# A decoder layer's weight preparation in one copy and one subtraction per 2048-column unit

## The chip, the core and the metric

The kernel runs on one core of a Trainium2 chip. The metric is the device time of one execution in microseconds. Times come from separate executions; the profile comes from one further execution, whose own time is given beside them.

## The reference

One decoder layer over 256 tokens with 2048 channels, in float32. Cut to what matters:

```python
proj = x @ w_in                       # 2048 -> GLA q,k,v,gate,rank | FoX q,k,v,forget | two merge gates
y_gla = gated_linear_attention(...) @ w_branch_gla        # 4 heads, chunked, RMSNorm, silu gate
y_fox = forgetting_attention(...) @ w_branch_fox          # 8 heads, softmax with log-forget bias
merged = sigmoid(ma) * y_gla + sigmoid(mb) * y_fox
x = layer_norm(ALPHA * x + merged @ w_out, ln1_g, ln1_b)
h = gelu(causal_dwconv(x @ w_gate, conv_w, conv_b)) * (x @ w_up)     # 2048 -> 5632
x = layer_norm(ALPHA * x + h @ w_down, ln2_g, ln2_b)                 # 5632 -> 2048
x = x + sigmoid(x @ w_ple_gate) * (p @ w_ple_proj)
```

All the large weights are read from HBM once, and all the large products have 256 rows.

## The kernel before, in words

**Arithmetic.** A float32 weight is not multiplied as it is. ScalarE (ACT) copies it into the fp32r type, which keeps fewer bits; this is `hi`. VectorE (DVE) subtracts `hi` from the raw weight; this is `lo`. TensorE (PE) then forms hi x activation-hi, hi x activation-lo and lo x activation-hi. Activations are split in the same way.

**Units.** The large weights are laid out as 284 units of 128 x 2048 float32 (1 MB), in the order in which PE uses them. `prep()` (L92) prepares the next unit: for each of its two halves of 1024 columns it takes a `raw` tile, issues the load on SyncE's queue (SP, L98), and has the half copied by ACT (L100, which the profile shows as L76, the line of the helper `copy`) and subtracted by DVE (L102). `unit()` (L110) hands the next unit to the matmuls after it has called `prep()` until the two units behind it are prepared too, so three units are in hand.

**The ring.** The pool `ring` holds `raw`, `hi` and `lo`. Before, each slot is half a unit: four slots of `raw`, six each of `hi` and `lo`. Two other kinds of tile use the raw slots: `maskf0` and `maskf1` at the start (L157; GpSimd, POOL, casts them into an 8-bit mask) and the four `praw` tiles of the embedding projection (`ple_prep`, L716). The first stage, the FoX value projection (`fv`, L285), has eight wider units of its own (`fv_prep`, L263: halves of 1048 columns), in the same three kinds of slots.

**Order.** SP's instructions, the loads, run in program order (L78). For the other engines a planner orders the instructions, by data dependence, slot release and priorities, when the kernel is built. The order on each engine can change with any edit. The engines then run their own streams in order and wait for one another by semaphores.

**Stages, in order of PE's work, with the tile that each writes:** `fv` (3 banks for each of two token blocks); `psfq`/`psfk`, `psq`/`psk` (units 0 to 31, one output block of 128 channels per unit or half unit), with the gate blocks `psg<head>` from `gla_gates` (L370) between; `gv` and `gr` (units 32 to 63; `x_half`, L213); `psm` (64 to 95); `psa`/`psb` (96 to 119); `wo` (120 to 135); `psg`/`psu` (136 to 223, the MLP's gate and up projections, L779); `dn` (224 to 267); `pg` (268 to 283). The stages `psfq` to `psb`, `psg` and `psu` go through `w_unit` (L163): per 128 columns of weight a 512-column matmul with `hi` (L169) and a 256-column one with `lo` (L171). `gv`, `gr`, `wo`, `dn`, `pg` go through `x_mm` (L186), with the weight as the moving operand. The output of such a stage is made in two halves of 1024 channels. PSUM has six banks for these stages (`pmm`) and two for transposes and small products (`pmx`).

**The seam after wo and dn.** The last two units of each are the tail: both are kept, and the four banks (two token blocks times two 512-column blocks) are finished one after another. As each ends, DVE adds the residual into `z` (L695) and takes statistics (L696). `ln_out` (L654) then combines the statistics (L659 to L662, with a power on POOL), normalises `z` in four parts (L667 on DVE, L670 on ACT), transposes them on PE into `ptl` (L673), applies gain and bias to each 128 x 128 block into `lny` (L680 on ACT and L682 on DVE in turn) and splits them into hi (L76) and lo (L685) of `x1T`, the next stage's activation. While this runs PE has the matmuls of the embedding projection, `pp` (`ple_proj`, L735). `affine` (L700) applies gain and bias (tiles `lnb`) to the untransposed `z` in 16 steps (L704, L706), between the MLP's units in program order.

**The middle of wo and dn.** `mid1` (L746) and `mid2` (L812) issue the loads of two `z` tiles and two `lnb` tiles, 1 MB each, on SP's queue between the loads of units; `ple_prep` issues the `praw` loads near the end of the same stages.

Of the kernel before, what the change touches and what calls it, by code (L numbers as in the profile page):

```python
# [9 lines left out]
F32 = mybir.dt.float32  # L10
F32R = mybir.dt.float32r
# [3 lines left out]
ALU = mybir.AluOpType  # L15
# [4 lines left out]
P = 128  # L20
# [12 lines left out]
NS = 1048  # L33
# [12 lines left out]
def tile_block(ctx: ExitStack, tc: tile.TileContext, wu, wfv, wpp, xT_in, x_in, pT_in, wlr,  # L46
               chan, gnorm, lng, ident_in, mask_in, cmask_in, sel_in, out):
    nc = tc.nc

    cst = ctx.enter_context(tc.tile_pool(name="cst", bufs=1))  # L50
    ring = ctx.enter_context(tc.tile_pool(name="ring", bufs=6))
    big = ctx.enter_context(tc.tile_pool(name="big", bufs=14))
    sm = ctx.enter_context(tc.tile_pool(name="sm", bufs=2))
    early = ctx.enter_context(ExitStack())
# [5 lines left out]
    def s8(shape, dt=F32, name=None):  # L60
        return big.tile(shape, dt, tag="S8", name=name)

    def t1(name):
        return sm.tile([P, 256], F32, tag="t1", bufs=6, name=name)

    def t2(name):
        return sm.tile([P, 512], F32, tag="t2", bufs=6, name=name)
# [7 lines left out]
    def copy(o, i, scale=1.0):  # L75
        nc.scalar.activation(o, i, AF.Copy, bias=0.0, scale=scale)  # L76
# [13 lines left out]
    ready = {}  # L90

    def prep():  # L92
        u = n_prep[0]
        n_prep[0] += 1
        his, los = [], []
        for h in range(2):
            raw = ring.tile([P, 1024], F32, tag="raw", bufs=4, name=f"raw{u}_{h}")
            nc.sync.dma_start(raw, wu[u, :, h * 1024:(h + 1) * 1024])  # L98
            hi = ring.tile([P, 1024], F32R, tag="hi", name=f"hi{u}_{h}")
            copy(hi, raw)  # L100
            lo = ring.tile([P, 1024], F32R, tag="lo", name=f"lo{u}_{h}")
            nc.vector.tensor_tensor(lo, raw, hi.bitcast(F32), ALU.subtract)  # L102
            his.append(hi)
            los.append(lo)
        ready[u] = (his, los)

    n_used = [0]
    NU = wu.shape[0]
# [1 line left out]
    def unit():  # L110
        u = n_used[0]
        n_used[0] += 1
        while n_prep[0] < min(NU, u + 3):
            prep()
        return ready.pop(u)
# [4 lines left out]
    def load_x(g, k0, k1, step=2):  # L120
        for k in range(k0, k1, step):
            e = slice(k, k + step)
            raw = t2("xraw").rearrange("p (k t) -> p k t", t=S)[:, 0:step, :]
            nc.sync.dma_start(raw, xT_in[:, 4 * g + k:4 * g + k + step, :])
            copy(xT[g][:, e, 0:256], raw)
            nc.vector.tensor_tensor(xT[g][:, e, 256:512], raw,
                                    xT[g][:, e, 0:256].bitcast(F32), ALU.subtract)
# [20 lines left out]
    def load_consts():  # L148
        nc.sync.dma_start(ident, ident_in)
        nc.sync.dma_start(chn, chan)  # L150
        nc.sync.dma_start(sel, sel_in)
        nc.sync.dma_start(cmask, cmask_in)

    def load_consts2():
        nc.sync.dma_start(gnb, gnorm.broadcast_to([P, 512]))
        for i in range(2):
            maskf = ring.tile([P, 4, 256], F32, tag="raw", bufs=4, name=f"maskf{i}")  # L157
            nc.sync.dma_start(maskf, mask_in[:, 8 * i:8 * i + 8, :].rearrange(
                "p (l t) n -> p l (t n)", t=2))
            nc.gpsimd.tensor_copy(mask[:, 4 * i:4 * i + 4, :], maskf)  # L160
# [99 lines left out]
    fch = ((0, 352), (352, 352), (704, 344))  # L260
    fbk = [[mmtile(f"fv_{t}{c}") for c in range(3)] for t in range(2)]

    def fv_prep(u, hs=(0, 1), his=None, los=None):  # L263
        his, los = his or [], los or []
        for h in hs:
            raw = ring.tile([P, NS], F32, tag="raw", bufs=4, name=f"fvraw{u}_{h}")
            hi = ring.tile([P, NS], F32R, tag="hi", name=f"fvhi{u}_{h}")
            lo = ring.tile([P, NS], F32R, tag="lo", name=f"fvlo{u}_{h}")
            for o, n in fch if u == 0 else ((0, NS),):
                e = slice(o, o + n)  # L270
                nc.sync.dma_start(raw[:, e], wfv[u, :, h, e])
                copy(hi[:, e], raw[:, e])
                nc.vector.tensor_tensor(lo[:, e], raw[:, e], hi[:, e].bitcast(F32), ALU.subtract)
            his.append(hi)
            los.append(lo)
        return his, los

    load_x(0, 0, 1, 1)
    f0 = fv_prep(0, (0,))
    load_x(0, 1, 2, 1)  # L280
    fvu = [fv_prep(0, (1,), *f0)]
    load_x(0, 2, 4)
    fvu.append(fv_prep(1))
    load_x(1, 0, 4)
    for u in range(8):  # L285
        hi, lo = fvu[u]
        for j in range(2):
            kt = 2 * u + j
            a = xT[kt // 4][:, kt % 4, :]
            for cs in ((0,), (1,), (2,)) if u == 0 else ((0, 1, 2),):  # L290
                for t in range(2):
                    ah, al = a[:, t * P:t * P + P], a[:, 256 + t * P:256 + t * P + P]
                    for i, (w, x) in enumerate(((hi[j], ah), (lo[j], ah), (hi[j], al))):
                        for c in cs:
                            o, n = fch[c]
                            nc.tensor.matmul(fbk[t][c][:, 0:n], lhsT=x, rhs=w[:, o:o + n],  # L296
                                             start=kt == 0 and i == 0,
                                             stop=kt == 15 and i == 2)
        if u + 2 < 8:
            fvu.append(fv_prep(u + 2))  # L300
        if u == 1:
            load_x(2, 0, 4)
        elif u == 2:
            load_x(3, 0, 4)
        elif u == 4:
            load_consts()
# [95 lines left out]
    fq = s8([P, 8, 256], name="fq")  # L402
    fk = s8([P, 8, 256], name="fk")
    load_consts2()
    for nm, dst, sc in (("fq", fq, P ** -0.5), ("fk", fk, 1.0)):
        for n in range(8):
            hi, lo = unit()
# [56 lines left out]
    for nm, dst, sc in (("q", gq, 1.0 / 16.0), ("k", gk, 1.0)):  # L464
        for n in range(8):
            hi, lo = unit()
            ps = mmtile(f"ps{nm}{n}")
            w_unit(ps, hi, lo, xT, range(16), True, True)
            h, c = n // 2, n % 2
# [141 lines left out]
    for n in range(32):  # L611
        hi, lo = unit()
# [14 lines left out]
    for n in range(16):  # L627
        hi, lo = unit()
# [5 lines left out]
        j = n % 2  # L634
# [81 lines left out]
    def ple_prep(half):  # L716

        w = [s8([P, 2048], F32R, name=f"pw{half}{i}") for i in range(2)]
        pt_ = s8([P, 2, 512], F32R, name=f"pTs{half}")
        pTs = [pt_[:, k, :] for k in range(2)]  # L720
        for k in range(2):
            raw = ring.tile([P, 1024], F32, tag="raw", bufs=4, name=f"praw{half}{k}")
            nc.sync.dma_start(raw, wpp[half, :, k * 1024:k * 1024 + 1024])
            o = slice(k * 1024, k * 1024 + 1024)
            copy(w[0][:, o], raw)
            nc.vector.tensor_tensor(w[1][:, o], raw, w[0][:, o].bitcast(F32), ALU.subtract)
        pT = t2("pTr").rearrange("p (k t) -> p k t", t=S)
        nc.sync.dma_start(pT, pT_in)
        for k in range(2):
            copy(pTs[k][:, 0:256], pT[:, k, :])  # L730
            nc.vector.tensor_tensor(pTs[k][:, 256:512], pT[:, k, :],
                                    pTs[k][:, 0:256].bitcast(F32), ALU.subtract)
        return w, pTs
# [20 lines left out]
    def done1(t):  # L754
        if t == 1:
            pb.extend(ple_proj(0, *pq[0]))
        ln_out(z1, st1, t, x1T, c_g1, c_b1, "l1", P_LN1[t])

    residual("wo", mT, 16, z1, st1, (mid1, lambda: pq.append(ple_prep(0))), done1)
    for t in range(2):  # L760
        for c in range(2):
# [17 lines left out]
    for n in range(NF):  # L779
        if n % 4 == 0:  # L780
            hT[n // 4] = (s8 if n < 40 else lt)([P, 4, 512], F32R, name=f"hT{n // 4}")
        hi, lo = unit()
# [15 lines left out]
        hi, lo = unit()  # L798
        psu = mmtile(f"psu{n}")
        w_unit(psu, hi, lo, x1T, range(16), True, True)  # L800
        u = t1("up")
# [18 lines left out]
    def done2(t):  # L820
        if t == 1:
            pb.extend(ple_proj(1, *pq[0]))
        ln_out(z2, st2, t, x2T, c_g2, c_b2, "l2", P_LN2[t])

    residual("dn", hT, NF, z2, st2, (mid2, lambda: pq.append(ple_prep(1))), done2)
    pp = [s8([P, 2, 1024], name=f"ppk{i}") for i in range(2)]
    for t in range(2):
# [116 lines left out]
```

## Time and profile before

| what | value |
|---|---|
| median of 3 runs | 1717.33 us (1717.16 to 1718.1) |
| profiled execution, its own time | 1717.8 us |
| its span | 1715.6 us |
| granted TensorE clock, mean | 0.998 |
| PE busy | 1704.6 us |
| DVE busy | 1093.3 us |
| ACT busy | 837.7 us |
| POOL busy | 37.7 us |
| DMA | 329.23 MB, mean 192 GB/s |

The span is the time from the first to the last instruction of the profiled execution; 2.2 us of its time lie outside. A row of a timeline gives start, busy us, engine, line, operation, output and inputs, the shape, the count of instructions merged in the row, and in brackets the idle time ahead of it and what ended it. A row of a group gives the count, the total busy us and the mean ns of one, and the idle time in front of them. A row of the waits gives the engine, what waited, for whom, the total us, the times and the longest. A row of the loads gives KB each and median us from issue to landing. Matmuls are pipelined, so their busy times overlap: the distance between starts is what one costs.

### The profile page before, as it was taken

Reading aid. Unit: us, or ns where it says so; the run is one execution under the profiler, and the core shown is the slowest. Engines: PE = TensorE matmul, PEld = TensorE weight load, DVE = VectorE, ACT = ScalarE, POOL = GpSimd, SP = SyncE. Lnnn points to the kernel's source line nnn. Section 1 sums busy time; section 2 is a strip of 40 time slices with the busy share of each in tenths; the row PEclk is TensorE's granted clock in tenths of the full one; section 3 lists DMA queues with packets and bytes.
Section 4 is the critical chain, followed back from the end, with each engine's and each line's share of the span. In section 5 each row is a group of like instructions: output and inputs, shape, how many; then the busy total and the mean of one; then the engine's idle time right before and its main releaser. Section 6 shows DMA issues by size and latency. Waiting matters only on the chain.

```text
span 1715.6 us, 23769 instructions
## 1 busy us (share of the span) xinstructions
PE 1704.6 (99%) x8997; PEld 1454.6 (85%) x8997; DVE 1093.3 (64%) x1580; ACT 837.7 (49%) x1209; POOL 37.7 (2%) x127
## 2 busy tenths in 40 slices
PE   9999999999999999999999999999999999999999
PEld 8988888888888888888878888888888888888787
DVE  6655677768755557774697666666766644544774
ACT  5744554445555544443374445445445433334633
POOL 1000000000000000000010000000000000000000
PEclk9999999999999999999999999999999999999999
DMA  8555455555554455557656555555555575555444
GB/s 304 203 205 173 152 169 177 176 173 172 181 175 160 161 192 187 188 192 276 221 175 218 189 192 186 192 188 186 194 186 190 190 282 192 181 196 197 160 173 171
DMA packets 91367, 329.23 MB, mean 192 GB/s; under 512 B 10309, under 2 KB 11973, under 8 KB 89973
## 3 DMA queue, kind: packets, MB, share of 16 engines
q1 hardware_dynamic: 90645, 324.57, 55.7%
q0 software_dynamic: 608, 3.15, 0.5%
q8 instruction: 70, 1.15, 0.3%
q14 instruction: 44, 0.36, 0.1%
HBM read 322.44 MB, written 5.24 MB: 191 GB/s over the span
## 4 chain that ended last, share of the span: by engine, by line
PE 98%; DVE 1%; DMA 0%; ACT 0%; SPq 0%; issue 0%; POOL 0%; ACTq 0%
PE dn L199 14%; PE psg L169 10%; PE psu L169 9%; PE psm L169 7%; PE gr L199 5%; PE gv L199 5%; PE wo L199 5%; PE pg L199 5%; PE psg L171 5%; PE psu L171 5%; PE psm L171 4%; PE psa L169 3%; PE fv L296 2%; PE psa L171 2%; PE psq L169 2%; PE psk L169 2%
## 5 line engine op out<-in xcount | busy, mean ns | idle before, releaser
L102 DVE TENSOR_TENSOR lo<-raw,hi 128x1024 fp32r<-128x1024 f32 x568 | 694.5, 1224 | 520.8 <-ACT hi L76 519.7
L76 ACT ACTIVATE hi<-raw 128x1024 fp32r<-128x1024 f32 x568 | 601.9, 1060 | 730.3 <-issue 254.3
L169 PE MATMUL psg<-x1T,hi 128*128 128x512 f32 x704 | 248.5, 394 | 0.0
L169 PE MATMUL psu<-x1T,hi 128*128 128x512 f32 x704 | 247.5, 393 | 0.0
L171 PE MATMUL psg<-x1T,lo 128*128 128x256 f32 x704 | 197.3, 280 | 0.0
L171 PE MATMUL psu<-x1T,lo 128*128 128x256 f32 x704 | 197.0, 280 | 0.0
L199 PE MATMUL dn<-hi,hT 128*128 128x512 f32 x704 | 193.8, 394 | 0.0
L169 PE MATMUL psm<-xT,hi 128*128 128x512 f32 x512 | 184.1, 402 | 0.0
L169 PEld LDWEIGHTS psg<-x1T,hi 128*128 128x128 f32 x704 | 132.9, 189 | 30.1
L199 PEld LDWEIGHTS dn<-hi,hT 128*128 128x128 f32 x704 | 132.1, 188 | 30.8
L169 PEld LDWEIGHTS psu<-x1T,hi 128*128 128x128 f32 x704 | 132.4, 188 | 30.0
L171 PE MATMUL psm<-xT,lo 128*128 128x256 f32 x512 | 143.4, 280 | 0.0
L171 PEld LDWEIGHTS psg<-x1T,lo 128*128 128x128 f32 x704 | 132.9, 189 | 0.1
L171 PEld LDWEIGHTS psu<-x1T,lo 128*128 128x128 f32 x704 | 132.5, 188 | 0.1
L169 PEld LDWEIGHTS psm<-xT,hi 128*128 128x128 f32 x512 | 96.3, 188 | 23.1 <-issue 1.0
L199 PE MATMUL dn<-lo,hT 128*128 128x512 f32 x352 | 111.3, 394 | 0.0
L171 PEld LDWEIGHTS psm<-xT,lo 128*128 128x128 f32 x512 | 96.5, 188 | 1.9 <-issue 1.9
L169 PE MATMUL psa<-oT,hi 128*128 128x512 f32 x256 | 90.1, 394 | 0.0
L199 PEld LDWEIGHTS dn<-lo,hT 128*128 128x128 f32 x352 | 66.1, 188 | 15.8
L199 PE MATMUL gr<-hi,xT 128*128 128x512 f32 x256 | 73.8, 399 | 0.0
L199 PE MATMUL gv<-hi,xT 128*128 128x512 f32 x256 | 73.6, 399 | 0.0
L171 PE MATMUL psa<-oT,lo 128*128 128x256 f32 x256 | 71.6, 280 | 0.0
(232 smaller groups left out, 2392.7 us busy)
## 6 DMA issues: line engine op xcount, KB each, us to landing
raw<-in_wu_dram SPq DMA_DIRECT2D x568, 512.0 KB, 3.6
fvraw<-in_wfv_dram SPq DMA_DIRECT2D x14, 524.0 KB, 6.7
lnb<-in_lng_dram SPq DMA_DIRECT2D x4, 1024.0 KB, 12.0
z<-in_x_dram SPq DMA_DIRECT2D x2, 1024.0 KB, 9.8
praw<-in_wpp_dram SPq DMA_DIRECT2D x4, 512.0 KB, 4.3
x1d<-z POOLq DMA_DIRECT2D x2, 1024.0 KB, 5.7
z<-x1d SPq DMA_DIRECT2D x2, 1024.0 KB, 6.4
xraw<-in_xT_dram SPq DMA_DIRECT2D x7, 256.0 KB, 7.0
```

The costliest lines, as they stand in the source:

```text
L76: nc.scalar.activation(o, i, AF.Copy, bias=0.0, scale=scale)
L102: nc.vector.tensor_tensor(lo, raw, hi.bitcast(F32), ALU.subtract)
L169: nc.tensor.matmul(ps, lhsT=hi[i // 8 if hoff == 0 else 0][:, w0 % 1024:w0 % 1024 + P], rhs=a[:, kt % 4, :], start=first and i == 0, stop= ...
L171: nc.tensor.matmul(ps[:, 256:512], lhsT=lo[i // 8 if hoff == 0 else 0][:, w0 % 1024:w0 % 1024 + P], rhs=a[:, kt % 4, 0:256], start=False, ...
L199: nc.tensor.matmul(bs[j][:, 0:m], lhsT=x, rhs=v[:, o:o + m], start=first and i == 0, stop=last and i == 2)
L296: nc.tensor.matmul(fbk[t][c][:, 0:n], lhsT=x, rhs=w[:, o:o + n], start=kt == 0 and i == 0, stop=kt == 15 and i == 2)
```

## The change: whole units instead of halves

`prep()` makes one copy of 2048 columns and one subtraction of 2048 columns for each unit, where it made two of each with 1024 columns. The two loads of 512 KB are kept. A slot of the ring is now a whole unit: two slots of `raw` and three each of `hi` and `lo`, which is the same memory. The `maskf` and `praw` tiles, and the fv stage's tiles, take slots of the same tags, so each takes the place of a whole unit; the fv stage still copies and subtracts by halves. The matmuls and their operands stay the same.

```diff
--- before.py
+++ after.py
@@ -48,7 +48,7 @@
     nc = tc.nc
 
     cst = ctx.enter_context(tc.tile_pool(name="cst", bufs=1))
-    ring = ctx.enter_context(tc.tile_pool(name="ring", bufs=6))
+    ring = ctx.enter_context(tc.tile_pool(name="ring", bufs=3))
     big = ctx.enter_context(tc.tile_pool(name="big", bufs=14))
     sm = ctx.enter_context(tc.tile_pool(name="sm", bufs=2))
     early = ctx.enter_context(ExitStack())
@@ -92,17 +92,15 @@
     def prep():
         u = n_prep[0]
         n_prep[0] += 1
-        his, los = [], []
+        raw = ring.tile([P, 2048], F32, tag="raw", bufs=2, name=f"raw{u}")
         for h in range(2):
-            raw = ring.tile([P, 1024], F32, tag="raw", bufs=4, name=f"raw{u}_{h}")
-            nc.sync.dma_start(raw, wu[u, :, h * 1024:(h + 1) * 1024])
-            hi = ring.tile([P, 1024], F32R, tag="hi", name=f"hi{u}_{h}")
-            copy(hi, raw)
-            lo = ring.tile([P, 1024], F32R, tag="lo", name=f"lo{u}_{h}")
-            nc.vector.tensor_tensor(lo, raw, hi.bitcast(F32), ALU.subtract)
-            his.append(hi)
-            los.append(lo)
-        ready[u] = (his, los)
+            e = slice(h * 1024, h * 1024 + 1024)
+            nc.sync.dma_start(raw[:, e], wu[u, :, e])
+        hi = ring.tile([P, 2048], F32R, tag="hi", name=f"hi{u}")
+        copy(hi, raw)
+        lo = ring.tile([P, 2048], F32R, tag="lo", name=f"lo{u}")
+        nc.vector.tensor_tensor(lo, raw, hi.bitcast(F32), ALU.subtract)
+        ready[u] = tuple([v[:, 0:1024], v[:, 1024:2048]] for v in (hi, lo))
 
     n_used = [0]
     NU = wu.shape[0]
@@ -154,7 +152,7 @@
     def load_consts2():
         nc.sync.dma_start(gnb, gnorm.broadcast_to([P, 512]))
         for i in range(2):
-            maskf = ring.tile([P, 4, 256], F32, tag="raw", bufs=4, name=f"maskf{i}")
+            maskf = ring.tile([P, 4, 256], F32, tag="raw", bufs=2, name=f"maskf{i}")
             nc.sync.dma_start(maskf, mask_in[:, 8 * i:8 * i + 8, :].rearrange(
                 "p (l t) n -> p l (t n)", t=2))
             nc.gpsimd.tensor_copy(mask[:, 4 * i:4 * i + 4, :], maskf)
@@ -260,37 +258,36 @@
     fch = ((0, 352), (352, 352), (704, 344))
     fbk = [[mmtile(f"fv_{t}{c}") for c in range(3)] for t in range(2)]
 
-    def fv_prep(u, hs=(0, 1), his=None, los=None):
-        his, los = his or [], los or []
+    def fv_prep(u, hs=(0, 1), got=None):
+        raw, hi, lo = got or (
+            ring.tile([P, 2, NS], F32, tag="raw", bufs=2, name=f"fvraw{u}"),
+            ring.tile([P, 2, NS], F32R, tag="hi", name=f"fvhi{u}"),
+            ring.tile([P, 2, NS], F32R, tag="lo", name=f"fvlo{u}"))
         for h in hs:
-            raw = ring.tile([P, NS], F32, tag="raw", bufs=4, name=f"fvraw{u}_{h}")
-            hi = ring.tile([P, NS], F32R, tag="hi", name=f"fvhi{u}_{h}")
-            lo = ring.tile([P, NS], F32R, tag="lo", name=f"fvlo{u}_{h}")
             for o, n in fch if u == 0 else ((0, NS),):
                 e = slice(o, o + n)
-                nc.sync.dma_start(raw[:, e], wfv[u, :, h, e])
-                copy(hi[:, e], raw[:, e])
-                nc.vector.tensor_tensor(lo[:, e], raw[:, e], hi[:, e].bitcast(F32), ALU.subtract)
-            his.append(hi)
-            los.append(lo)
-        return his, los
+                nc.sync.dma_start(raw[:, h, e], wfv[u, :, h, e])
+                copy(hi[:, h, e], raw[:, h, e])
+                nc.vector.tensor_tensor(lo[:, h, e], raw[:, h, e], hi[:, h, e].bitcast(F32),
+                                        ALU.subtract)
+        return raw, hi, lo
 
     load_x(0, 0, 1, 1)
     f0 = fv_prep(0, (0,))
     load_x(0, 1, 2, 1)
-    fvu = [fv_prep(0, (1,), *f0)]
+    fvu = [fv_prep(0, (1,), f0)]
     load_x(0, 2, 4)
     fvu.append(fv_prep(1))
     load_x(1, 0, 4)
     for u in range(8):
-        hi, lo = fvu[u]
+        _, hi, lo = fvu[u]
         for j in range(2):
             kt = 2 * u + j
             a = xT[kt // 4][:, kt % 4, :]
             for cs in ((0,), (1,), (2,)) if u == 0 else ((0, 1, 2),):
                 for t in range(2):
                     ah, al = a[:, t * P:t * P + P], a[:, 256 + t * P:256 + t * P + P]
-                    for i, (w, x) in enumerate(((hi[j], ah), (lo[j], ah), (hi[j], al))):
+                    for i, (w, x) in enumerate(((hi[:, j], ah), (lo[:, j], ah), (hi[:, j], al))):
                         for c in cs:
                             o, n = fch[c]
                             nc.tensor.matmul(fbk[t][c][:, 0:n], lhsT=x, rhs=w[:, o:o + n],
@@ -719,7 +716,7 @@
         pt_ = s8([P, 2, 512], F32R, name=f"pTs{half}")
         pTs = [pt_[:, k, :] for k in range(2)]
         for k in range(2):
-            raw = ring.tile([P, 1024], F32, tag="raw", bufs=4, name=f"praw{half}{k}")
+            raw = ring.tile([P, 1024], F32, tag="raw", bufs=2, name=f"praw{half}{k}")
             nc.sync.dma_start(raw, wpp[half, :, k * 1024:k * 1024 + 1024])
             o = slice(k * 1024, k * 1024 + 1024)
             copy(w[0][:, o], raw)
```

## The prediction

> **What bounds the kernel now.** I read the page first (busy times, then the chain that ended last), then the waits of PE.
>
> ```profile
> PE 1704.6 (99%) x8997; PEld 1454.6 (85%) x8997; DVE 1093.3 (64%) x1580; ACT 837.7 (49%) x1209; POOL 37.7 (2%) x127
> PE 98%; DVE 1%; DMA 0%; ACT 0%; SPq 0%; issue 0%; POOL 0%; ACTq 0%
> PE ptl L673 <- ACT lny L680: 3.1, 2, 2.2
> PE fv L296 <- ACT fvhi L76: 1.1, 1, 1.1
> PE ptl L673 <- DVE z L667: 1.1, 2, 0.6
> ```
>
> The span is 1715.6 us and PE carries 98% of it. The three largest waits of PE (line waited for, total us, times, longest) come to 5.3 us in the whole kernel. PE's idle time is 1715.6 - 1704.6 = 11.0 us. The change alters no matmul, so a gain can't be larger than these 11 us and what PE runs slowly behind its waits (some 2 us, part 3). DVE and ACT have hundreds of idle microseconds, so time saved on them is worth nothing unless PE waits for it. What can move the end is therefore one thing: places where PE comes to wait for a prepared weight, or for something queued behind a preparation.
>
> **Part 1, the two longer instructions.** These are the groups of the page, two shorter forms of each engine, and the issues of the loads.
>
> ```profile
> L102 DVE TENSOR_TENSOR lo<-raw,hi 128x1024 fp32r<-128x1024 f32 x568 | 694.5, 1224 | 520.8 <-ACT hi L76 519.7
> L76 ACT ACTIVATE hi<-raw 128x1024 fp32r<-128x1024 f32 x568 | 601.9, 1060 | 730.3 <-issue 254.3
> L604 DVE TENSOR_TENSOR oT<-gt,oT 128x512 fp32r<-128x512 f32 x8 | 5.5, 682 | 0.7 <-ACT oT L76 0.7
> L76 ACT ACTIVATE x1T<-lny 128x512 fp32r<-128x512 f32 x8 | 4.9, 628 | 0.0
> raw<-in_wu_dram SPq DMA_DIRECT2D x568, 512.0 KB, 3.6
> lnb<-in_lng_dram SPq DMA_DIRECT2D x4, 1024.0 KB, 12.0
> z<-x1d SPq DMA_DIRECT2D x2, 1024.0 KB, 6.4
> ```
>
> No 2048-column form stands in the trace. For DVE, 512 to 1024 columns adds 1.224 - 0.682 = 0.54 us, so 2048 columns would be 1.224 + 2 x 0.54 = 2.30 us; bounds are 1.22 (it can't be less than half of itself) and twice 1.224 = 2.45. For ACT the step is 1.060 - 0.628 = 0.43, so 1.060 + 0.86 = 1.92 us, between 1.06 and 2.12. I take 2.30 and 1.92, on the straight line through the two rows. That saves 284 x (2.45 - 2.30) = 43 us of DVE and 284 x (2.12 - 1.92) = 57 us of ACT, and by the paragraph above nothing of the time.
>
> **Part 2, the ring of whole units in the steady state.** PE's period is the spacing of its pairs here; psg before 877 is slow and is used further down.
>
> ```profile
> 875.03 0.78 PE L169 MATMUL psg<-x1T,hi 128*128 128x512 f32 x1
> 875.61 0.41 PE L171 MATMUL psg<-x1T,lo 128*128 128x256 f32 x1
> 875.82 0.63 PE L169 MATMUL psg<-x1T,hi 128*128 128x512 f32 x1
> 877.09 0.40 PE L169 MATMUL psg<-x1T,hi 128*128 128x512 f32 x1
> 877.44 0.39 PE L169 MATMUL psu<-x1T,hi 128*128 128x512 f32 x1
> 877.67 0.28 PE L171 MATMUL psu<-x1T,lo 128*128 128x256 f32 x1
> 877.79 0.39 PE L169 MATMUL psu<-x1T,hi 128*128 128x512 f32 x1
> ```
>
> A pair takes 877.79 - 877.44 = 0.35 us and a unit has 16, so 5.6 us per unit. With three whole slots, hi of unit u+3 may start once PE has left unit u; hi and lo are there 1.92 + 2.30 + about 0.1 = 4.3 us later, and PE wants them 2 x 5.6 = 11.2 us later: 6.9 us to spare. The raw slots go round thus: load, hi, lo, next load, with 11.2 us for each round. Both halves of a unit are sent together, and the nearest rows are 3.6 us for 512 KB alone and 6.4 us for 1 MB as one; the estimate is 3.6 us and 1.5 us for the second half at twice the mean rate, 5.1 us. So 5.1 + 1.9 + 2.3 + 0.2 = 9.5 us, by the 6.4 row 10.8. Either end is under 11.2, so the steady state loses nothing. The 12.0 row is a load with others ahead of it in the queue, and stands for part 5. What hides the longer instructions is the 6.9 us; an engine that is busy elsewhere for longer uncovers them. That happens where stages meet.
>
> **Part 3, the start (fv to fq).** The order of DVE, ACT and PE comes from the planner, and the instruction streams of the two built programs differ here. Rows of before on POOL, ACT and PE:
>
> ```profile
> 41.59 1.65 POOL L160 CAST mask<-maskf 128x1024 uint8<-128x1024 f32 x1 [37.20 <-DMA maskf<-in_mask_dram]
> 44.16 1.04 POOL L160 CAST mask<-maskf 128x1024 uint8<-128x1024 f32 x1 [0.92 <-DMA maskf<-in_mask_dram]
> 45.47 1.06 ACT L76 ACTIVATE hi<-raw 128x1024 fp32r<-128x1024 f32 x1 [4.72 <-DMA raw<-in_wu_dram]
> 51.94 0.47 ACT L76 ACTIVATE fv<-fv 128x352 f32<-128x352 f32 x1 [5.41 <-PE fv L296]
> 54.17 0.98 ACT L76 ACTIVATE fv<-fv 128x352 f32<-128x352 f32 x2
> 55.17 2.07 ACT L76 ACTIVATE hi<-raw 128x1024 fp32r<-128x1024 f32 x2
> 53.65 0.47 PE L169 MATMUL psfq<-xT,hi 128*128 128x512 f32 x1
> 65.99 0.40 PE L169 MATMUL psfq<-xT,hi 128*128 128x512 f32 x1
> ```
>
> Before, the first half of unit 0 was copied at 45.47, ahead of the copies that empty the fv banks, so PE began psfq at 53.65 and stood at the third bank's first matmul at 65.99. After, maskf0 and maskf1 fill both raw slots, each 512 KB in a slot of 1 MB; unit 0 can be loaded only after POOL's cast of 41.59, and in the built order hi of unit 0 stands behind all the fv copies. It so takes the place of the row at 55.17: hi0 55.17 to 57.1, lo0 57.1 to 59.4, hi1 57.1 to 59.0, lo1 59.4 to 61.7. PE's order is the hi matmul of both banks, then lo0, so psfq flows from about 59.5. Two units of 5.6 us less what has run put the third bank at 70.3: **+4.3 us** against 65.99. Bounds: +2 if PE finds more to do while it waits, +6 if loads come later.
>
> Behind that stall lies a second cost. In the rows at 875 PE came from waits of 2.2 and 0.9 us: the pair from 875.03 to 875.82 took 0.79 us instead of 0.35, and full speed was back by 877.09, so some 1.5 to 2 us are lost after such waits. I add **+1.0** at the start, half because this stall lies between matmuls that still run. The Trainium skill ("TensorE: Matmul & The Clock Gate", Part 1) says that PE falls to half clock after an idle window of about 3.4 us and needs about as long to come back. The trace agrees on the half speed, 0.79 against 0.35, but there the waits were shorter than that. By the page's figure the estimate for a 5 us stall would be 1.7 us instead of 1.0.
>
> **Part 4, LN1 (end of wo to psg).** Rows of ACT, DVE and PE of before:
>
> ```profile
> 850.52 1.06 ACT L76 ACTIVATE hi<-raw 128x1024 fp32r<-128x1024 f32 x1 [1.72 <-PE wo L199]
> 856.82 0.69 DVE L696 BATCH_NORM_STATS2 st<-z 128x6 f32<-128x512 f32 x1
> 857.55 0.26 DVE L659 BATCH_NORM_AGGREGATE mv<-st 128x2 f32<-128x24 f32 x1
> 858.79 0.54 DVE L667 TENSOR_SCALAR z<-z,mv 128x512 f32<-128x512 f32 x1
> 861.85 0.68 DVE L704 TENSOR_TENSOR z<-z,lnb 128x512 f32<-128x512 f32 x1
> 862.47 1.23 DVE L102 TENSOR_TENSOR lo<-raw,hi 128x1024 fp32r<-128x1024 f32 x1
> 866.54 0.68 DVE L685 TENSOR_TENSOR x1T<-lny,x1T 128x512 fp32r<-128x512 f32 x1
> 868.25 0.73 DVE L682 TENSOR_SCALAR lny<-ptl,chn 128x128 f32<-128x128 f32 x2
> 872.72 0.66 PE L673 MATMUL ptl<-ident,z 128*128 128x128 f32 x4 [2.19 <-ACT lny L680]
> 874.26 1.12 PE L673 MATMUL ptl<-ident,z 128*128 128x128 f32 x4 [0.89 <-ACT lny L680]
> ```
>
> The copy at 850.52 waited for PE to leave unit 133's second half, so the last two units of wo (the tail) begin at S = 850.4, and psg began at 875.03 = S + 24.6. Before, the normalising of rows 0 to 127 began at 857.55, under the tail. After, DVE's order from the second bn_stats (end before S + 7.1; about S + 8.5 after, as ten instead of six projection matmuls stand ahead) to the last x1T piece that psg's first matmul needs is: three whole lo (units 136 to 138), two evacuations of z and two statistics (4 x 0.68), two z normalisings, 12 lny pieces, 8 affine steps on z, 5 x1T pieces and six short steps. With the rows above: 3 x 2.30 + 4 x 0.68 + 2 x 0.54 + 12 x 0.36 + 8 x 0.65 + 5 x 0.65 + 6 x 0.2 = 6.9 + 2.7 + 1.1 + 4.3 + 5.2 + 3.3 + 1.2 = 24.7 us. The evacuations wait some 1.6 us for the last bank of wo. So psg begins at 8.5 + 24.7 + 1.6 = S + 34.8, or S + 35.2 with the changes between engines: **+10.5 us**. Before had, in the same stretch, three half lo (3.7 us) and one affine step: 3.2 us of the loss are preparations and 4.6 are affine steps that the planner put ahead, the rest are waits. Bounds: +5 if the lo, the affine steps and the wait overlap with PE's projection matmuls, +14 if each of ACT's preparations (hi137 and hi138 stand ahead of the normalising and of the lny pieces) adds its 1.92 us too. The slow restart exists before as well; a longer one adds **+0.7**.
>
> **Part 5, the other seams.** LN2 has the same parts, but its built order keeps the statistics of the first rows ahead of lo, so I give it **+1.0** (0 to 4). At the middle of wo and of dn, 4 MB (two z, two gains, the 12.0 us row) stand ahead of a raw load:
>
> ```profile
> 803.08 1.06 ACT L76 ACTIVATE hi<-raw 128x1024 fp32r<-128x1024 f32 x1 [7.17 <-DMA raw<-in_wu_dram]
> ```
>
> ACT waited 7.17 us there and PE nothing. The whole unit arrives about 1.5 us after its first half and takes 4.2 us instead of 2.3; that uses up the cover, and lo of unit 129 comes behind the evacuations: **+1.0** for both (0 to 4). The praw loads each take a raw slot: **+0.5** (0 to 2). Where gv, gr, wo, dn and pg go from one half to the other, a 2.3 us lo stands ahead of a short step that PE wants: **+1.0** for five seams (0 to 4).
>
> **The sum.** 4.3 + 1.0 + 10.5 + 0.7 + 1.0 + 1.0 + 0.5 + 1.0 = 20.0 us. The profiled execution took 1717.8 us (span 1715.6 and 2.2 around it), 0.5 above the median of 1717.33, so the median comes to **1737.3 us**, 1.2% slower.
>
> **The rivals.** *Seams covered (no change).* The planner's order is worth less than I read: PE has the projection matmuls to run under LN1, and the start's stall is filled. For it speaks that PE lost only 5.3 us before with the same chains; against it, that these chains end exactly at PE (the waits at 872.72 and 874.26). It gives the rows' lower bounds with nothing else, within 3.4 us of 1717.3. Within 0.2% is about what a measurement of this kernel can tell from no change. Chance 0.06.
>
> *Shorter chains (faster).* At LN1 and the start the same work is done by fewer instructions, and if whole-unit steps fall behind the normalising instead of ahead, PE's 5.3 us of waits and the slow restart (1.5 to 2 us) go: 1717.3 - 7 = 1710. It decides where lo137 falls against the lny pieces; in the built order it falls ahead. Chance 0.05.
>
> *The raw ring becomes the bound (much slower).* If a round of a raw slot takes over 11.2 us, every unit takes half a round. The load would have to take 6.8 us; the single 1 MB row has 6.4. At a round of 12 us a unit takes 6.0 instead of 5.6, so 284 x 0.4 = 114 us, 1831 us. Against it speaks that before ran four 512 KB slots at 3.6 us. Chance 0.06.
>
> *The change does nothing.* The built program has 284 pairs of 2048-column instructions, so this is out.
>
> **How the numbers follow.** The forecast, slower by the seams, has 0.83. Adding the lower bounds gives 2 + 5 = 7 us, 1724; the upper 6 + 2 + 14 + 1 + 4 + 4 + 2 + 4 = 37, 1754. Not all terms err the same way, but terms that I have not seen can only add: 1723 to 1755 holds this case, and leaves out the three rivals, 0.17 together. Faster by over 0.2%: 0.05. Within: 0.06. Slower: 0.83 + 0.06 = 0.89.
>
> **What would show it.** The 2048-column groups at 2.30 and 1.92 us, 284 each. PE's waits some 20 us instead of 6, with psfq behind hi and lo of units 0 and 1, and psg some 10 us later against the end of wo. PE's period of 5.6 us in the long stages unchanged. It would be wrong if PE waited for lo or hi throughout a stage, or if the stretch from 850.4 to psg were not longer.

## The result, and the profile after

The changed kernel takes 1736.22 us (median of 4 runs, 1735.75 to 1737.16) against 1717.5 us for the kernel before (4 runs): a ratio of 1.011, 95% interval 1.0094 to 1.0126. Its profiled execution took 1736.3 us; its span is 1734.4 us, 18.8 us longer than before. From the page of the changed kernel: busy times, the chain that ended last, the two groups of preparations, the loads.

```profile
PE 1710.2 (99%) x8997; PEld 1460.9 (84%) x8997; DVE 1060.9 (61%) x1296; ACT 785.2 (45%) x925; POOL 34.1 (2%) x127
PE 92%; DVE 3%; DMA 2%; ACT 1%; issue 1%; SPq 0%; POOL 0%; POOLq 0%; ACTq 0%; DVEq 0%
L102 DVE TENSOR_TENSOR lo<-raw,hi 128x2048 fp32r<-128x2048 f32 x284 | 650.6, 2291 | 496.9 <-ACT hi L76 496.7
L76 ACT ACTIVATE hi<-raw 128x2048 fp32r<-128x2048 f32 x284 | 544.5, 1917 | 602.4 <-PE psu L167 147.8
raw<-in_wu_dram SPq DMA_DIRECT2D x568, 512.0 KB, 4.6
```

The two engines that prepare weights did save work: DVE 694.5 - 650.6 = 43.9 us, ACT 601.9 - 544.5 = 57.4 us. None of it shows in the time. PE's part of the chain fell from 98% to 92%, and what took its place is DVE, ACT and the loads. PE's idle time rose from 11.0 to 1734.4 - 1710.2 = 24.2 us; its busy time rose by 5.6 us with the same matmuls, at a mean granted clock of 0.993 instead of 0.998. PE runs slowly behind its stalls, as shown below for the start. Four groups of PE's waits, at the places treated below (line waited for, total us, times, longest); all of PE's waits add up to 19.8 us, where they were 6.7 before:

```profile
PE ptl L670 <- ACT lny L677: 10.5, 4, 5.5
PE psfq L167 <- ACT hi L76: 1.8, 2, 1.5
PE pg L197 <- ACT hi L76: 1.5, 1, 1.5
PE pg L197 <- DVE lo L102: 1.1, 1, 1.1
```

To see where the time went, one compares when PE reaches the same matmul in both timelines. First before, then after: the end of psfq, the start of wo, the end of the MLP's projections (psu), a matmul in the middle of pg (the fifth of the bank pg_11b), and the last matmul. The lag is the time in the changed kernel less the time before.

```profile
99.87 0.28 PE L171 MATMUL psfq<-xT,lo 128*128 128x256 f32 x1
772.30 0.63 PE L199 MATMUL wo<-hi,mT 128*128 128x512 f32 x2
1366.77 0.28 PE L171 MATMUL psu<-x1T,lo 128*128 128x256 f32 x1
1671.46 0.28 PE L199 MATMUL pg_11b<-lo,x2T 128*128 128x256 f32 x1
1711.09 0.28 PE L199 MATMUL pg_11b<-hi,x2T 128*128 128x256 f32 x1
```

```profile
106.18 0.28 PE L169 MATMUL psfq<-xT,lo 128*128 128x256 f32 x1
776.89 0.63 PE L197 MATMUL wo<-hi,mT 128*128 128x512 f32 x2
1380.29 0.28 PE L169 MATMUL psu<-x1T,lo 128*128 128x256 f32 x1
1685.91 0.28 PE L197 MATMUL pg_11b<-lo,x2T 128*128 128x256 f32 x1
1729.88 0.28 PE L197 MATMUL pg_11b<-hi,x2T 128*128 128x256 f32 x1
```

| place | PE's lag behind the kernel before, us | lost there, us |
|---|---|---|
| end of psfq (the start) | 6.31 | +6.3 |
| start of wo (700 us of steady stages) | 4.59 | -1.7 |
| end of psu (wo, LN1 and the MLP) | 13.52 | +8.9 |
| middle of pg (dn, LN2 and the first half of pg) | 14.45 | +0.9 |
| end of pg | 18.79 | +4.3 |

Three places lose 19.5 us, the long stages between them gain some, and LN2 loses a little: the lag is 12.92 ahead of dn's tail (1601.7 in the kernel before) and 14.58 in the first half of pg (1642.3). **At the start**, in ACT's, DVE's and PE's timelines:

```profile
54.92 1.91 ACT L76 ACTIVATE hi<-raw 128x2048 fp32r<-128x2048 f32 x1
56.87 4.50 DVE L102 TENSOR_TENSOR lo<-raw,hi 128x2048 fp32r<-128x2048 f32 x2 [0.88 <-ACT hi L76]
58.99 0.80 PE L167 MATMUL psfq<-xT,hi 128*128 128x512 f32 x1 [1.49 <-ACT hi L76]
59.59 0.41 PE L169 MATMUL psfq<-xT,lo 128*128 128x256 f32 x1
59.80 0.63 PE L167 MATMUL psfq<-xT,hi 128*128 128x512 f32 x1
60.44 0.63 PE L167 MATMUL psfq<-xT,hi 128*128 128x512 f32 x1
63.64 0.54 PE L167 MATMUL psfq<-xT,hi 128*128 128x512 f32 x1
```

hi of unit 0 stands behind fv's copies, where it was forecast (54.92 for 55.17), and psfq flows from 59.6. Then PE runs at little over half speed, 60.44 - 59.80 = 0.64 us for a pair instead of 0.35, until 63.6. The granted clock is 0.50 from 59.0 to 63.6.

**At the end of wo and LN1**: SP, ACT, DVE and PE of the changed kernel. Before, the first bank of the tail was emptied at 853.30, and the row of it stands first.

```profile
853.30 0.69 DVE L695 SCALAR_TENSOR_TENSOR z<-z,wo 128x512 f32<-128x512 f32 x1 [0.46 <-PE wo L199]
```

```profile
839.86 6.58 SPq L720 DMA_DIRECT2D praw<-in_wpp_dram  x2
849.83 1.06 ACT L76 ACTIVATE pw<-praw 128x1024 fp32r<-128x1024 f32 x1 [5.12 <-DMA praw<-in_wpp_dram]
853.72 1.92 ACT L76 ACTIVATE hi<-raw 128x2048 fp32r<-128x2048 f32 x1 [2.21 <-DMA raw<-in_wu_dram]
854.85 1.09 PE L197 MATMUL pp<-pw,pTs 128*128 128x512 f32 x4
856.72 1.53 PE L197 MATMUL pp<-pw,pTs 128*128 128x512 f32 x6
857.43 1.92 ACT L76 ACTIVATE hi<-raw 128x2048 fp32r<-128x2048 f32 x1 [1.79 <-DMA raw<-in_wu_dram]
863.18 0.69 DVE L692 SCALAR_TENSOR_TENSOR z<-z,wo 128x512 f32<-128x512 f32 x1 [1.51 <-PE wo L197]
865.83 2.28 DVE L102 TENSOR_TENSOR lo<-raw,hi 128x2048 fp32r<-128x2048 f32 x1
878.52 1.97 PE L670 MATMUL ptl<-ident,z 128*128 128x128 f32 x8 [5.47 <-ACT lny L677]
887.10 1.97 PE L670 MATMUL ptl<-ident,z 128*128 128x128 f32 x8 [2.32 <-ACT lny L677]
888.73 0.80 PE L167 MATMUL psg<-x1T,hi 128*128 128x512 f32 x1
```

Two things are to be seen. The first bank is emptied 863.18 - 776.89 = 86.3 us after the start of wo; before it was 853.30 - 772.30 = 81.0. So LN1 begins 5.3 us late: the praw loads wait for whole raw slots, and the last two units of wo are copied at 853.72 and 857.43. PE fills part of the gap with ten projection matmuls (`pp`), some 2.3 us, which before ran only from 863.56 on; these 2.3 us are moved, not lost. And from that bank to psg it takes 888.73 - 863.18 = 25.6 us against 875.03 - 853.30 = 21.7 before, 3.8 us more.

**In the second half of pg**: SP, ACT and PE.

```profile
1681.88 4.32 SPq L847 DMA_DIRECT2D out_dram<-res  x4
1686.31 10.48 SPq L98 DMA_DIRECT2D raw<-in_wu_dram  x6
1691.72 1.91 ACT L76 ACTIVATE hi<-raw 128x2048 fp32r<-128x2048 f32 x1 [9.18 <-DMA raw<-in_wu_dram]
1693.68 1.06 PE L197 MATMUL pg<-hi,x2T 128*128 128x512 f32 x4 [1.46 <-ACT hi L76]
1696.01 1.22 PE L197 MATMUL pg<-lo,x2T 128*128 128x512 f32 x2 [1.14 <-DVE lo L102]
```

The four stores of pg's first half wait for DVE's results and stand on SP's queue ahead of the load of unit 278. That load goes out at 1686.31; 5.4 us of loading, 1.9 of copying and 2.3 of subtracting later PE has the whole unit, and it has been waiting. Its two waits come to 2.6 us. The granted clock is 0.88 in the 14 us from 1686, where it was 1.00 before in the same work (1671 to 1685), and 14 x 0.12 = 1.7 us make up the rest of the 4.3. Before, the stores stood ahead of the load too, but the first half of the unit was loaded and copied alone, and PE did not wait.

### The profile page after: what moved, and what is told of

Read it like the earlier page. It is cut to its first block, busy times and chain, and to the rows that moved or that the text cites. A ratio compares the mean times of both kernels' runs of the same rounds, so it can differ in the third digit from the quotient of the medians.

```text
span 1734.4 us, 22721 instructions
## 1 busy us (share of the span) xinstructions
PE 1710.2 (99%) x8997; PEld 1460.9 (84%) x8997; DVE 1060.9 (61%) x1296; ACT 785.2 (45%) x925; POOL 34.1 (2%) x127
## 4 chain that ended last, share of the span: by engine, by line
PE 92%; DVE 3%; DMA 2%; ACT 1%; issue 1%; SPq 0%; POOL 0%; POOLq 0%; ACTq 0%; DVEq 0%
PE dn L197 12%; PE psg L167 9%; PE psu L167 9%; PE psm L167 7%; PE wo L197 5%; PE gv L197 5%; PE gr L197 5%; PE psg L169 5%; PE psu L169 5%; PE psm L169 3%; PE psa L167 3%; PE pg L197 2%; PE fv L293 2%; DMA raw<-in_wu_dram 2%; PE psfq L167 2%; PE psa L169 2%
## 5 line engine op out<-in xcount | busy, mean ns | idle before, releaser
L102 DVE TENSOR_TENSOR lo<-raw,hi 128x2048 fp32r<-128x2048 f32 x284 | 650.6, 2291 | 496.9 <-ACT hi L76 496.7
L76 ACT ACTIVATE hi<-raw 128x2048 fp32r<-128x2048 f32 x284 | 544.5, 1917 | 602.4 <-PE psu L167 147.8
L197 PE MATMUL pg<-hi,x2T 128*128 128x512 f32 (+1 forms) x256 | 70.1, 383 | 2.0 <-ACT hi L76 1.5
```

What stands on the lines that cost most here:

```text
L197: nc.tensor.matmul(bs[j][:, 0:m], lhsT=x, rhs=v[:, o:o + m], start=first and i == 0, stop=last and i == 2)
```

## The experiments

Theory 1 put the losses down to the length of one preparation, which holds DVE and ACT for 2.3 and 1.9 us and gives PE the first half of a unit late. Theory 2 put them down to the slots: whole raw slots that mask and praw tiles occupy. All medians are of 4 to 11 runs beside 7 to 18 of the kernel before on the same chip.

**Half steps in whole slots.**

```diff
-        copy(hi, raw)
-        nc.vector.tensor_tensor(lo, raw, hi.bitcast(F32), ALU.subtract)
+        for h in range(2):
+            e = slice(h * 1024, h * 1024 + 1024)
+            copy(hi[:, e], raw[:, e])
+            nc.vector.tensor_tensor(lo[:, e], raw[:, e], hi[:, e].bitcast(F32), ALU.subtract)
```

> The ring stays in whole units (two raw slots, three hi, three lo), but each unit is again copied and subtracted in two steps of 1024 columns. Theory 1 (the losses come from the length of one preparation: it blocks DVE and ACT at the seams, and the first half of a unit is ready later): the built order at LN1 is again like that of before, so the 9 us lost there go; the last stage (pg), where PE waited for hi and lo of a unit whose load came late, gets its first half some 2 us sooner and loses 1 to 3 us instead of 4.6; at the start the first half of unit 0 is copied ahead of the copies of fv, so 0 to 4 of the 6.3 us stay. Sum: 1718 to 1724 us. Theory 2 (the losses come from the size of the slots: loads wait for whole slots): 1730 us or more, with PE's waits as in the changed kernel.

Measured: 1715.53 us, ratio 0.9988 (0.9979 to 0.9998). All of the loss is gone, and a little more. The slots by themselves cost nothing; each of the three losses needs the whole-unit step. The order at LN1 is like before's again, and PE waits there as before:

```profile
PE ptl L672 <- ACT lny L679: 2.9, 2, 2.6
PE ptl L672 <- DVE z L666: 1.6, 2, 1.0
```

The next runs keep the whole steps and take the places one by one.

**Units 0 and 1 ahead of the masks.**

```diff
+    prep()
+    prep()
     load_consts2()
```

> The changed kernel, but the loads and preparations of units 0 and 1 are issued ahead of the two mask loads, so the masks wait for the slots of units 0 and 1 and not the other way round. Theory 1 (PE's stall at the start is unit 0, late because the mask tiles fill both raw slots and because its copy then stands behind the copies of fv): the 6.3 us at the start go but for 0 to 1.5 us, 1730 to 1731.5 us, nothing else moves. Rival (whichever takes the slots, a unit is late): unit 2, whose slot is now behind a mask, stalls PE by 3 to 5 us instead: 1733 to 1736 us.

Measured: 1731.93 us, ratio 1.0088 (1.0073 to 1.0103), 4.3 less than the changed kernel. The start's loss is gone altogether: wo begins ahead of the kernel before (772.30), so 6.4 us were gained by there in the profiled execution.

```profile
770.52 0.63 PE L197 MATMUL wo<-hi,mT 128*128 128x512 f32 x2
PE wo L197 <- ACT hi L76: 0.8, 1, 0.8
PE pg L197 <- ACT hi L76: 1.8, 1, 1.8
```

That execution took 1734.55 us, the slowest of the four. In it 2.1 of the 6.4 us went again by the end of psu, with PE now waiting for hi at the end of wo, and 2.5 more by the end of pg; by the median 4.3 us stayed.

**The first stores of pg on POOL's queue.**

```diff
-            nc.sync.dma_start(out[t, :, o], r[:, e])
+            (nc.gpsimd if nh == 0 else nc.sync).dma_start(out[t, :, o], r[:, e])
```

> The changed kernel, but the four stores of the first half of pg are issued from POOL's queue and not from SP's, so that no load of a unit stands behind them. Theory 1 (the 4.6 us lost in pg come from SP: the stores wait for the last evacuation and hold the load of unit 278, which then needs 1.9 us of copy and 2.3 us of subtraction before PE has all of it): PE's waits in pg go, 1731 to 1732 us. Rival (PE waits in pg because DVE is busy with evacuations): 1 us or less is gained, 1735 us or more.

Measured: 1734.05 us, ratio 1.0099 (1.0084 to 1.0114). Pg no longer waits for hi or lo, and its loss shrinks from the 5.9 us between pg's first and last matmul to 1.1. The 4.3 us of the second half are gone, so the place and its cause are shown. But the sum fell by 2.2 us only, because at the end of wo, where the instructions of the two programs are the same, a tail unit was copied 7.8 us after its load's issue instead of 6.5, and PE waited:

```profile
PE wo L197 <- ACT hi L76: 1.8, 1, 1.8
```

The tail of wo has no margin left in the changed kernel, so a load that is a microsecond late costs the time.

**LN1: affine steps and preparations of units 137 and 138 pinned behind it**, and then **the affine steps alone**.

```diff
+        pin = tc.keep_in_program_order if u in (137, 138) else (lambda i: i)
-        copy(hi, raw)
+        pin(nc.scalar.activation(hi, raw, AF.Copy, bias=0.0, scale=1.0))
...
-        while n_prep[0] < min(NU, u + 3):
+        while n_prep[0] < min(NU, u + (2 if u == 135 else 3)):
...
-                nc.vector.tensor_tensor(zc, zc, gb_[0][:, g * 512:g * 512 + 512], ALU.mult)
+                tc.keep_in_program_order(
+                    nc.vector.tensor_tensor(zc, zc, gb_[0][:, g * 512:g * 512 + 512], ALU.mult))
```

Not shown here: the subtraction and the second affine step (the addition) are pinned in the same way. The run with both also calls for unit 137 one unit later; the run with the affine steps alone has only the pinned affine steps.

> The changed kernel with the seam after wo alone changed: the affine steps on z, and hi and lo of units 137 and 138, are pinned behind the LN1 steps that stand ahead of them in the program. Theory 1 (psg starts late because DVE runs 2 whole lo and 8 affine steps, 9.8 us, between the steps of LN1 that PE waits for, and ACT two whole hi): the 8.7 us lost there fall to -1 to +2: 1726.5 to 1729.5 us. Rival (the loss is that the tail of wo ends later, as ten instead of six projection matmuls stand ahead of it and LN1 begins later): 2 us at most are gained, 1734 us or more.

> The changed kernel, with only the affine steps on z pinned behind the DVE steps that stand ahead of them in the program; the preparations stay where the planner puts them. Theory 1 (at LN1 PE waits for DVE's serial work, and 8 affine steps of 0.65 us are 5.2 us of it): psg starts 3 to 4 us sooner and nothing comes late for it, since no preparation is moved: 1732 to 1733.5 us. Rival (the loss at LN1 is the later end of wo's tail and whole lo alone): 1 us or less, 1735 us or more.

Measured: 1738.14 us with both (ratio 1.0123, 1.0107 to 1.0138) and 1738.72 us with the affine steps alone (1.0121, 1.0106 to 1.0136). Both expectations failed. PE's timeline with both pinned, then with the affine steps alone:

```profile
884.65 0.79 PE L168 MATMUL psg<-x1T,hi 128*128 128x512 f32 x1
892.32 0.49 PE L168 MATMUL psu<-x1T,hi 128*128 128x512 f32 x1 [0.74 <-ACT hi L101]
894.12 0.79 PE L168 MATMUL psg<-x1T,hi 128*128 128x512 f32 x1 [1.30 <-ACT hi L101]
```

```profile
888.74 0.80 PE L167 MATMUL psg<-x1T,hi 128*128 128x512 f32 x1
```

With both, psg begins at 884.65 instead of 888.73, as theory 1 wants. But units 137 and 138 have to be prepared at some time: PE then waits for them, restarts slowly, and by the end of psu the 4.1 us are gone (lag 14.1 for 13.5). With the affine steps alone psg begins at 888.74, as if nothing had been moved. In the changed kernel DVE stands still for only 0.34 us between the first bank of the tail and psg. Without the eight affine steps there it stands still for 3.9 us: the steps had filled time in which DVE would have waited for ACT and PE. PE's waits for lny stayed (11.6 us for 10.5). From the first bank to psg it takes 25.1 us with the affine steps alone and 21.3 with both, about as before (21.7), so it is the preparations that stretch LN1.

**praw two units earlier**, and **one of the two steps halved**.

```diff
-            x_half(f"{name}{nh}", act, K, ev, tail=2 if nh == 1 else 0, mid=(mid[nh], 4 if nh == 0 else K // 2 - 5),
+            x_half(f"{name}{nh}", act, K, ev, tail=2 if nh == 1 else 0, mid=(mid[nh], 4 if nh == 0 else K // 2 - 7),
```

> The changed kernel, with the two praw tiles loaded two units earlier in the second half of wo and of dn. Theory 2 (a good part of the loss at LN1 is that the praw tiles hold a raw slot just ahead of the tail, so that hi and lo of units 134 and 135 come late, the first bank is emptied 5.4 us later than its share, and the projection matmuls are used up ahead of the tail): the first evacuation comes 2 to 5 us sooner against the start of wo, and 2 to 5 us are gained: 1731 to 1734 us. Theory 1 (the steps that DVE runs between those of LN1): 1 us or less, 1735 us or more.

```diff
-        nc.vector.tensor_tensor(lo, raw, hi.bitcast(F32), ALU.subtract)
+        for h in range(2):
+            e = slice(h * 1024, h * 1024 + 1024)
+            nc.vector.tensor_tensor(lo[:, e], raw[:, e], hi[:, e].bitcast(F32), ALU.subtract)
```

> Whole-unit slots and one copy of 2048 columns on ACT, but two subtractions of 1024 columns on DVE. If the length of DVE's step costs the time (it blocks the chain of LN1, where DVE is the engine that works without a pause): 6 us or more of the 9 at LN1 come back, the start keeps its 6 us and pg 2 to 4: 1725 to 1729 us. If the length of ACT's step does it (nothing of a unit may be subtracted before all of it is copied): 1732 us or more.

```diff
-        copy(hi, raw)
+        for h in range(2):
+            e = slice(h * 1024, h * 1024 + 1024)
+            copy(hi[:, e], raw[:, e])
```

> The counterpart: two copies of 1024 columns on ACT, one subtraction of 2048 columns on DVE. If DVE's step costs the time: LN1 keeps 6 us or more of its 9, the start loses 2 to 4 us less (half of unit 0 is copied ahead of fv's copies): 1729 to 1734 us. If ACT's step does it: 1725 us or less.

Measured: praw earlier 1739.52 us (ratio 1.0126, 1.0111 to 1.0142); half subtractions 1738.25 us (1.0122, 1.0105 to 1.0139); half copies 1733.45 us (1.0092, 1.0077 to 1.0107). Praw earlier fails: the first bank is emptied 87.1 us after the start of wo, no sooner than the 86.3 of the changed kernel. That the ring hadn't caught up by then is a reading that no run tests. By the time alone the halved steps settle little: by the run with half subtractions ACT's step would decide, by the one with half copies DVE's. The second also missed its forecast for the start, where the loss stayed (psfq's last matmul at 105.95 instead of 106.18).

The traces say more if the seam is split at the first bank, and if runs are compared that have equally many projection matmuls behind it. With 14 of them there, from the first bank to psg it takes 25.6 us in the changed kernel and 22.1 with half subtractions. With 23 or 24 it takes 27.2 with whole steps (the run with the three places together, below), 24.2 with half copies and 22.0 with both halved. These are single executions, but either engine's half step takes some 3 us off, so the whole steps of both delay psg.

Ahead of the first bank neither helps much: it is emptied 91.4 us after the start of wo with half subtractions, 85.4 with half copies, 81.7 with both. With half subtractions PE waited three times for a whole hi in wo. The 91.4 has to be read with care, as the 86.3 of the changed kernel became 87.7 and 89.2 in the runs on units 0 and 1 and on pg's stores, which left this seam alone. Why the tail of wo takes both halves is open.

**praw off the ring.**

```diff
-        for k in range(2):
-            raw = ring.tile([P, 1024], F32, tag="raw", bufs=2, name=f"praw{half}{k}")
-            nc.sync.dma_start(raw, wpp[half, :, k * 1024:k * 1024 + 1024])
-            o = slice(k * 1024, k * 1024 + 1024)
+        for k in range(4):
+            o = slice(k * 512, k * 512 + 512)
+            raw = t2("praw")
+            nc.sync.dma_start(raw, wpp[half, :, o])
```

> The changed kernel, but the praw tiles are loaded in four pieces of 512 columns into another pool's tiles and take no raw slot (four copies and four subtractions of 512 columns in place of two of each of 1024). Theory 2 (the tail of wo is late because the two praw tiles cost the raw ring a round of some 10 us that gives PE no unit, with 1 us of margin in each other round to make it up): the first evacuation of the tail comes at 81 to 83 us after the start of wo, as before, instead of 86.3, and the time falls by 4 to 5 us: 1731 to 1732.5 us. What is left at LN1, some 4 us from the evacuation to psg, is whole lo and hi among LN1's steps. Rival (the tail is late because of whole units as such): 1 us or less, 1735 us or more.

Measured: 1731.47 us, ratio 1.0084 (1.0068 to 1.0099). In its DVE and PE timelines:

```profile
857.85 0.69 DVE L692 SCALAR_TENSOR_TENSOR z<-z,wo 128x512 f32<-128x512 f32 x1 [2.03 <-PE wo L197]
776.60 0.63 PE L197 MATMUL wo<-hi,mT 128*128 128x512 f32 x2
```

857.85 - 776.60 = 81.3 us: LN1 begins as early as before. By the medians 4.8 us are gained, at both seams together, since dn's praw tiles left the ring too. At LN1 psg comes 3.6 us sooner against the kernel before (lag 10.1 instead of 13.7), less than the first bank, because the projection matmuls stand behind that bank again. Theory 2 is right about the tail, with whole steps as its condition, since the same slots with half steps lose nothing.

**The three places together, and the best version.** The first takes the edits of units 0 and 1, praw and the stores on top of the changed kernel. The second takes praw and the stores on top of the half steps in whole slots.

> The changed kernel with the three edits together: units 0 and 1 ahead of the masks, the praw tiles off the ring, the first stores of pg off SP's queue; the preparations remain whole. If the three places are the causes and independent, 6.4 us (start), 4 to 5 us (tail of wo) and 4.7 us (pg) come off 1736.2: 1720 to 1721.5 us, and 3 to 4 us stay that only shorter steps at LN1 take away. If one stall only moves to the next place, as in the run with the units first, 1725 us or more.

> The kernel with whole-unit slots and half steps (1715.5 us), with the praw tiles off the ring and the first stores of pg off SP's queue as well. It has no stall left at these places by its profile, so no gain is forecast: 1714.5 to 1716 us. It shows whether whole slots with half steps stay ahead of the kernel before.

Measured: 1722.33 us (ratio 1.0026, 1.0015 to 1.0037) and 1714.82 us (0.9982, 0.9973 to 0.9991). Of the 18.7 us of loss the three edits take 13.9; the forecast of 1720 to 1721.5 was a little too good. The rest is LN1. In the DVE and PE timelines of the first:

```profile
851.90 0.69 DVE L694 SCALAR_TENSOR_TENSOR z<-z,wo 128x512 f32<-128x512 f32 x1 [1.90 <-PE wo L197]
879.14 0.79 PE L167 MATMUL psg<-x1T,hi 128*128 128x512 f32 x1
```

From the first evacuation to psg it is 27.2 us against 21.7 before. The second has the same praw tiles and stores but half steps, and there it is 873.08 - 851.25 = 21.8 us:

```profile
851.25 0.68 DVE L694 SCALAR_TENSOR_TENSOR z<-z,wo 128x512 f32<-128x512 f32 x1
873.08 0.78 PE L169 MATMUL psg<-x1T,hi 128*128 128x512 f32 x1
```

So the whole steps among those of LN1 cost these 5.4 us. (The two also differ in the order of units 0 and 1, which is long past by then.) The second is the fastest kernel of the study, 0.18% ahead of before; its interval overlaps that of the half steps alone, so the two edits on top aren't shown to help.

## Why the prediction was right, and where its terms were not

The forecast was 1737.3 us and 1.2% slower, measured were 1736.22 and 1.1%. The mechanism was right: PE came to wait for whole-unit steps where stages meet, its waits were forecast at some 20 us and came to 19.8, and the long stages lost nothing. The closeness of the total is in part luck, since terms that were too high met terms that were too low:

| place | forecast, us | measured, us |
|---|---|---|
| start, with the slow restart | +5.3 | +6.3 |
| wo's tail and LN1 (10.5, 0.7 and the praw's 0.5) | +11.7 | +8.9 |
| middles of wo and dn | +1.0 | 0.2 at wo (part of the 8.9), none at dn |
| LN2 | +1.0 | +1.7 |
| five seams between halves | +1.0 | +4.3, all in pg and by another cause |
| long stages | 0 | -1.7 up to wo, -0.6 in dn |

- **Durations and steady state.** 2.30 and 1.92 us were forecast for the straight line through two rows, 2.291 and 1.917 measured. The rival in which the ring becomes the bound is out, although the load of a half rose from 3.6 to 4.6 us.
- **The start.** The stall was right to some 0.2 us; the slow restart was mis-sized. It lasted from 59.0 to 63.6, seven pairs in 4.65 us where 0.35 each would be 2.45: 2.2 us instead of 1.0. The loss that the term was taken from was misread too: the three pairs from 875.03 to 877.09 took 2.06 us in place of 1.05, so 1.0 us was lost there and not 1.5 to 2. The Trainium skill ("TensorE: Matmul & The Clock Gate", Part 1) gives half clock after an idle window of about 3.4 us and some 3.4 us to return. This trace shows 4.6 us of slow pairs at a granted clock of 0.50, after a stretch in which PE was not idle throughout and no single wait was longer than 1.5 us. The estimate by the page, 1.7, was nearer than the term taken.
- **LN1.** Whole steps among those of LN1 do delay psg, but the split was wrong. The affine steps, 4.6 us of the sum, cost nothing (psg at 888.74 without them). The sum of DVE's instructions was taken for the length of the chain; the count was right and DVE did run almost without a gap, but the affine steps stood in time that PE and ACT needed anyway, since LN1 goes to and fro between PE, ACT and DVE. The praw slots, priced at +0.5 (0 to 2), cost 4.8 us at both seams, as their removal shows. The step that failed there is the margin: a round of a raw slot of 9.5 to 10.8 us against 11.2 carries the ring in the steady state. That it doesn't recover a round that brings PE no unit is how the removal is read here; the rounds themselves were not measured.
- **Pg.** Its 4.3 us were not seen. The prediction looked for what stands ahead of a raw load at the middles of wo and dn, and not at pg, where the stores stand there. Its term of 1.0 for five seams had pg among them, but for a whole lo ahead of a short step. This miss and the one at praw made up for the affine steps.
- **Rivals.** Covered seams and shorter chains are out: PE's waits rose from 6.7 to 19.8 us. Savings of 101 us on two engines off the path bought nothing. The first of these rivals was tied to the lower bounds of the terms, but these add up to 7 us and it was counted within 3.4.
- **Small slips.** The three waits of PE that were called the largest leave out one of 1.2 us at the program's start (tile `warm_ps`). Half a megabyte at twice the mean rate is 1.4 us and not 1.5. Neither changes a term by more than 0.2 us.

## What to carry to other kernels

Merging two instructions on engines that PE did not wait for saved no time here, and made each result later and each turn on the engine longer. Before such a merge, look for the places where the ring has to start, restart or share its slots, and price the merged step there. A ring with a round just under its period worked here until other tiles took its slots; count such guests as whole rounds. And for each load on an ordered queue, look at what stands ahead of it, stores included. Last, split a seam at a matmul or an evacuation that both timelines have: the time of the whole run hid that either half step helps behind the first bank.

## What the runs showed of the hardware that was not expected

Whole slots with half steps beat half slots with half steps by 2.0 us (0.9988, 0.9979 to 0.9998). In its timeline PE gains 0.5 us by the end of psfq, as its wait for fvhi fell from 1.1 to 0.4 us, and 1.9 us more by the start of wo, a little in each stage and without a wait that went away; the changed kernel gains 1.7 us over the same stages. What shortens PE's stages isn't shown.

PE slowed down without a long pause: from 53.3 to 57.0 us of the changed kernel it was busy for 1.84 of 3.70 us at a granted clock of 1.00, from 57.0 to 59.0 for 0.51 of 2.00 us at 0.53, and its next 4.6 us, without a pause, ran at 0.50.

In two programs with the same instructions up to pg, 6.5 us lay between the issue of a load and the copy in one and 7.8 us in the other, at the same place, which decided whether PE waited.
